# Moving 32 tokens of a mixture-of-neurons layer from gathered rows to dense products, and making fewer products ahead

## Chip, cores and metric

The kernel runs as one program on one core of a Trainium2 chip. The metric is the device time of one execution in microseconds (us), and the median over several executions is what is compared. Engines are named as in the profile: PE (TensorE matmuls), PEld (its weight loads), DVE (VectorE), ACT (ScalarE), POOL (GpSimd), SP (SyncE, which issues most DMAs).

## What is computed

Two layers of a diffusion backbone over 512 latent tokens (`x`) and 256 context tokens (`ctx`), width 1024, all in fp32. Each layer is a token mixer and then a channel mixer, "PEER", which is all that matters here. PEER picks for every token 8 x 16 = 128 of 16,384 single-neuron experts; each has a row `u` and a row `v` of 1024 numbers:

```python
qr = (h @ wq)...;  scores = einsum(qr, subkeys)        # 8 heads x 2 halves x 128 keys
s1, i1 = top_k(scores[..., 0, :], 16);  s2, i2 = top_k(scores[..., 1, :], 16)
top, pos = top_k(s1 + s2, 16)                          # of 256 pairs; expert = i1 * 128 + i2
gate = softmax(top)
act = gelu(einsum('ted,td->te', u[ek], hk))            # ek: the 128 experts of a token
y   = einsum('te,ted->td', gate * act, v[ek])
```

The first layer does this for latent and context tokens, the second for the latent tokens alone, since nothing reads its context stream afterwards.

## The kernel before, in words

Tokens stand in blocks of 128. In each layer `peer` (line 664 and on) treats some tokens as *dense* and some as *gathered*.

**Dense tokens.** For them the activations of all 16,384 experts are computed: for every pair of two 128-expert blocks (64 pairs in all), `experts_in` loads two tiles of `u`, splits each into a rounded high part (`whi`, ACT, L298) and a rest (`wlo`, DVE, L300), makes three products for each of 8 slices of the width (`mm3`, L307 to L309; 2 x 8 x 3 = 48 matmuls for a pair, whose moving operand is as wide as there are dense tokens) and applies gelu (ACT, L805). In `dense`, 16 groups of 8 expert blocks follow each other: for a group the activations `A` are multiplied by the gates (DVE, L829), split (ACT L832, DVE L833), and for each of 8 slices of the output a tile of `v` is loaded, split (L298, L300) and multiplied in 24 matmuls (L840 to L842; 192 a group), whose sum DVE adds to the residual (L844). So a layer has 64 x 48 = 3072 U matmuls and 16 x 192 = 3072 V matmuls.

The gates of dense tokens are a table, 16,384 x tokens, built in `gates` and written to memory (`gd`). A *quad* is 32 tokens of it: per token, ACT and DVE make two one-hot matrices (L775 to L786), PE multiplies them (L791, which the trace shows as two instructions each), ACT copies the result out (L792). `dense` reads the table back (`gt`, L818).

While the table is being built, `ahead(q)` computes, after each quad, some of the U products and writes their activations to memory (`ad`, L726); `dense` reads those back (L821) instead of computing them. `AHEAD` says how many of the 64 pairs are made ahead in each layer, and `AHEAD_SET` spreads them from pair 3 up to pair `SPAN`. The first three pairs (`FIRST`) are computed only after the last gate matmul (`issue_after(self.last_gate)`).

**Gathered tokens.** `gather_block` (L866 and on) fetches, for a block of tokens on 128 partitions, one expert row for each partition with an indirect DMA from POOL (L881, 512 KB each), first all `u` rows, each reduced against the token's own `h` on DVE (L888), then all `v` rows, each multiplied and added to `acc` (L897). At the end PE transposes `acc` and DVE adds it to the residual (L903 to L907). The buffers `gr` (3) and `gs` (1) hold rows in flight; the first 96 `u` rows of a block whose picks come early use `gr` alone.

In the second layer 352 tokens are dense (`nt = len(db) * P - r`, `r = REST[1] = 32`), the block of the last 128 tokens is gathered with 128 u and 128 v fetches, and the 32 tokens left over are gathered in a second, packed block: four groups of 32 partitions hold the same 32 tokens with a quarter of their experts each, so that 32 u and 32 v fetches do. In the first layer all 512 latent tokens are dense and the 256 context tokens gathered.

**What sets the order.** The program is written in the order above; a scheduler places every engine's instructions by a simulation of its own when the kernel is built, and each engine then runs its list in that fixed order. All DMAs but the gathers are issued by SP, in order.

```python
for i in range(q * n_ahead // n, (q + 1) * n_ahead // n):   # ahead(q); n = nt // 32 quads
    A = self.experts_in(l, ap, hx, AHEAD_SET[l][i], nt)
    nc.sync.dma_start(ad[i], A)
...
nq = (nt - n * P) // 32
self.gates(kp, gd, n, ahead, *sel, min(nq, P // 32))
...
if r:
    self.gather_block(l, cp, c2, hdx[0, P - r:], *rest, TC + nt, r, 0)
```

Of the kernel before, what the change touches and what calls it, by code (L numbers as in the profile page):

```python
# [32 lines left out]
TINY = 2.0 ** -60  # L33
HUGE = 1.0e37
WPRIO = 400
AHEAD = (36, 40)
SPAN = (39, 60)
FIRST = 3
AHEAD_SET = [[FIRST + i * (m - FIRST) // n for i in range(n)] for n, m in zip(AHEAD, SPAN)]
ND = 3  # L40
REST = (0, 32)
STEP = (-1, -1)
POOL_NM = False
U0 = 96
# [12 lines left out]
class Kern:  # L57
# [603 lines left out]
    def peer(self, l):  # L661
# [3 lines left out]
        db = [b for b in range(NCB, NB) if b not in gb]  # L665
        r = REST[l]
        nt = len(db) * P - r
        early = EARLY[l]
        with ExitStack() as es:
            dr = self.pool(f"dr{l}", stack=es, space=DRAM)  # L670
            gd = dr.tile([P // 4, P, nt // 32, 4, 32], F, name="gd")
            n_ahead = AHEAD[l]
            ad = dr.tile([n_ahead, P, 2, nt], F, name="ad")
# [330 lines left out]
```

## Time and profile before

| | us |
|---|---|
| median of 3 runs (lowest 4182.07, highest 4183.38) | 4182.8 |
| the profiled execution | 4198.16 |
| its span in the trace | 4196.4 |

| engine | busy us | share of the span |
|---|---|---|
| PE | 3905.2 | 93% |
| PEld | 3359.6 | 80% |
| DVE | 3399.4 | 81% |
| ACT | 1794.3 | 43% |
| POOL | 1391.9 | 33% |

The profiled execution took 15.4 us (0.4%) more than the median; all times that are read from the trace are its own. Times below are us from the start of the span. The second layer's channel mixer fills about the last 1,230 us of it: U products begin at about 2975, the table of gates is built from about 3070 to 3390, the dense groups run from there to 4158, and a final norm ends the span. A share of PE's busy time hides gaps between pipelined matmuls, so the steps from one matmul's start to the next's are read as well.

### The profile page before, as it was taken

The page shows a single profiled execution, that of the slowest core. Times are in us where ns is not written, and L with a number is a line of the kernel's source. Part 1 is how long each engine was busy: PE and PEld are TensorE (multiplying, and loading weights), DVE is VectorE, ACT ScalarE, POOL GpSimd, SP SyncE. Part 2 cuts the span into 40 slices and gives each one's busy share as a digit, 9 for nine tenths or more (in the row PEclk, how much of TensorE's full clock was granted, in tenths as well). Part 3 has the DMA queues.
Part 4 walks back from the last instruction along what each step waited for, and adds up shares of the span by engine and source line. Part 5 has one row for each costly group of instructions (what it writes and reads, how often), then busy time and mean ns, then how long its engine had stood idle before and what let it go on. Part 6 is the DMA issues. An engine that isn't in the chain of part 4 may idle for free. (4 is left out here: it accounts for less than half of the span.)

```text
span 4196.4 us, 59194 instructions
## 1 busy us (share of the span) xinstructions
PE 3905.2 (93%) x21317; PEld 3359.6 (80%) x21317; DVE 3399.4 (81%) x6491; ACT 1794.3 (43%) x3096; POOL 1391.9 (33%) x1020
## 2 busy tenths in 40 slices
PE   8999999989999999999999879988999999998898
PEld 5888779778888778877777658866899998888897
DVE  4766639989886999988888868757999888898897
ACT  4444332358985222222222335433387853333332
POOL 0211112033331335455555532212013333444443
PEclk8999999999999999999999989989999999999998
DMA  6444122389998899988899921112469999999996
GB/s 222 138 155 156 64 74 74 114 291 318 313 314 278 295 337 344 338 317 310 317 323 319 321 96 58 64 61 88 138 218 315 325 368 337 342 333 344 349 338 232
DMA packets 391173, 1021.28 MB, mean 243 GB/s; under 512 B 32096, under 2 KB 159328, under 8 KB 386528
## 3 DMA queue, kind: packets, MB, share of 16 engines
q1 hardware_dynamic: 271072, 581.24, 39.9%
q0 software_dynamic: 119808, 436.26, 29.3%
q8 instruction: 168, 2.75, 0.3%
q14 instruction: 125, 1.02, 0.1%
HBM read 918.00 MB, written 99.35 MB: 242 GB/s over the span
## 5 line engine op out<-in xcount | busy, mean ns | idle before, releaser
L298 ACT ACTIVATE whi<-wraw 128x1024 fp32r<-128x1024 f32 x624 | 656.5, 1058 | 1160.8 <-PE p L841 465.4
L881 POOL DMA_INDIRECT gr<-in_u,picki x360 | 486.9, 1353 | 968.0 <-DVE gr L888 640.9
L300 DVE TENSOR_TENSOR wlo<-wraw,whi 128x1024 fp32r<-128x1024 f32 x592 | 721.2, 1223 | 96.9 <-ACT whi L298 92.5
L840 PE MATMUL p<-Wh,whi 128*128 128x512 f32 (+1 forms) x2048 | 730.5, 364 | 46.2 <-ACT Wh L832 22.3
L841 PE MATMUL p<-Wl,whi 128*128 128x512 f32 (+1 forms) x2048 | 741.5, 363 | 26.1 <-DVE Wl L833 25.9
L842 PE MATMUL p<-Wh,wlo 128*128 128x512 f32 (+1 forms) x2048 | 740.5, 364 | 24.5 <-DVE wlo L300 23.4
L309 PE MATMUL p<-hxh,wlo 128*128 128x512 f32 (+1 forms) x2048 | 744.7, 364 | 9.3 <-DVE wlo L300 9.2
L307 PE MATMUL p<-hxh,whi 128*128 128x512 f32 (+1 forms) x2048 | 744.1, 363 | 3.0 <-ACT whi L298 2.6
L308 PE MATMUL p<-hxl,whi 128*128 128x512 f32 (+1 forms) x2048 | 743.3, 363 | 0.0
L881 POOL DMA_INDIRECT gr<-in_v,picki x312 | 443.5, 1421 | 469.4 <-DVE acc L897 359.5
L888 DVE SCALAR_TENSOR_TENSOR gr<-gr,htok 128x1024 f32<-128x1024 f32 x360 | 436.4, 1219 | 118.8 <-DMA gr<-in_u,picki 117.4
L840 PEld LDWEIGHTS p<-Wh,whi 128*128 128x128 f32 x2048 | 389.8, 192 | 100.9 <-ACT Wh L832 29.5
L842 PEld LDWEIGHTS p<-Wh,wlo 128*128 128x128 f32 x2048 | 392.2, 192 | 80.5 <-DVE wlo L300 40.4
L841 PEld LDWEIGHTS p<-Wl,whi 128*128 128x128 f32 x2048 | 393.4, 192 | 77.1 <-DVE Wl L833 36.3
L897 DVE SCALAR_TENSOR_TENSOR acc<-gr,gw,acc 128x1024 f32<-128x1024 f32 x308 | 394.1, 1280 | 54.0 <-DMA gr<-in_v,picki 51.6
L309 PEld LDWEIGHTS p<-hxh,wlo 128*128 128x128 f32 x2048 | 388.9, 190 | 50.3 <-DVE wlo L300 12.9
L307 PEld LDWEIGHTS p<-hxh,whi 128*128 128x128 f32 x2048 | 388.7, 190 | 42.1 <-ACT whi L298 4.1
L308 PEld LDWEIGHTS p<-hxl,whi 128*128 128x128 f32 x2048 | 388.8, 190 | 37.7
L832 ACT ACTIVATE Wh<-A 128x1024 fp32r<-128x1024 f32 (+1 forms) x128 | 118.1, 926 | 386.4 <-DVE A L829 305.1
L791 PEld LDWEIGHTS gps<-oA,oB 128*128 128x128 f32 x1728 | 240.2, 194 | 44.6 <-ACT oB L780 13.5
L791 PE MATMUL gps<-oA,oB 128*128 128x128 f32 x1728 | 251.3, 280 | 25.4 <-DVE oA L783 13.8
L307 PE MATMUL pj<-h512h,whi 128*128 128x512 f32 x640 | 261.9, 412 | 12.4 <-ACT h512h L368 3.2
(320 smaller groups left out, 6703.4 us busy)
## 6 DMA issues: line engine op xcount, KB each, us to landing
wraw<-in_ut SPq DMA_DIRECT2D x256, 512.0 KB, 6.2
wraw<-in_vt SPq DMA_DIRECT2D x256, 512.0 KB, 6.2
gd<-stg SPq DMA_DIRECT2D x27, 2048.0 KB, 13.5
wmod<-in_w_mod SPq DMA_DIRECT2D x96, 512.0 KB, 4.7
wraw<-in_w_in SPq DMA_DIRECT2D x64, 512.0 KB, 3.5
gt<-gd SPq DMA_DIRECT2D x32, 1024.0 KB, 8.3
gt<-gd SPq DMA_DIRECT2D x32, 704.0 KB, 7.8
ad<-A SPq DMA_DIRECT2D x36, 512.0 KB, 6.8
```

The source lines that it names most:

```text
L298: nc.scalar.activation(hi, raw, AF.Copy)
L300: (eng or nc.vector).tensor_tensor(lo, raw, hi.bitcast(F), op=OP.subtract)
L307: nc.tensor.matmul(out, wh[:, k], ah[:, k, :n], start=i == 0, stop=False)
L308: nc.tensor.matmul(out, wh[:, k], al[:, k, :n], start=False, stop=False)
L309: nc.tensor.matmul(out, wl[:, k], ah[:, k, :n], start=False, stop=i == KC - 1)
L791: mm = nc.tensor.matmul(pt[:, s], B[:, s4 + s], A[:, s4 + s], start=True, stop=True)
L840: nc.tensor.matmul(pt, hi[:, j], wh, start=j == 0, stop=False)
L841: nc.tensor.matmul(pt, hi[:, j], wl, start=False, stop=False)
L842: nc.tensor.matmul(pt, lo[:, j], wh, start=False, stop=j == NG - 1)
L881: nc.gpsimd.indirect_dma_start(out=t, out_offset=None, in_=src, in_offset=bass.IndirectOffsetOnAxis(ap=eidx[:, e:e + 1], axis=0))
L888: nc.vector.scalar_tensor_tensor(u, u, 1.0, htok, op0=OP.mult, op1=OP.mult, accum_out=act[:, e:e + 1])
L897: nc.vector.scalar_tensor_tensor(acc, v, w[:, e:e + 1], acc, op0=OP.mult, op1=OP.add)
```

## The change

`REST[1]` goes from 32 to 0: the second layer has 384 dense tokens (three whole blocks), 12 quads of gates and no packed second block of gathers. `AHEAD` goes from 36 and 40 pairs to 34 and 30, and the first layer's `SPAN` from 39 to 37, so that its pairs made ahead are 3 to 36 and no longer 3 to 38.

```diff
-AHEAD = (36, 40)
-SPAN = (39, 60)
+AHEAD = (34, 30)
+SPAN = (37, 60)
 FIRST = 3
 AHEAD_SET = [[FIRST + i * (m - FIRST) // n for i in range(n)] for n, m in zip(AHEAD, SPAN)]
 ND = 3
-REST = (0, 32)
+REST = (0, 0)
```

The numbers move instructions at three places that matter below.

PE, second layer, end of the building of gates (`p_...` are U products for pairs, `gps` the gate products). Before, with 40 pairs ahead, the last products of the table stand among U products:

```order
L791 MATMUL gps<-oA,oB 128x128 x2
L309 MATMUL p_28526<-hxh,wlo 128x352
L791 MATMUL gps<-oA,oB 128x128
L307 MATMUL p_28526<-hxh,whi 128x352
L791 MATMUL gps<-oA,oB 128x128 x4
L308 MATMUL p_28526<-hxl,whi 128x352
```

Now the last pair made ahead ends before them, and 128 tokens' products, four quads, stand in one piece:

```order
L307 MATMUL p_27988<-hxh,whi 128x384
L308 MATMUL p_27988<-hxl,whi 128x384
L309 MATMUL p_27988<-hxh,wlo 128x384
L761 MATMUL gtr<-ident,ix 128x128
L761 MATMUL gtr<-ident,gate 128x128
L791 MATMUL gps<-oA,oB 128x128 x128
L307 MATMUL p_28061<-hxh,whi 128x384
```

The U products behind that piece are those of the first three pairs, which wait for the last gate. Counted along the two lists, 33.0 pairs stood before the 256th token's product and 40 before the 352nd; now 29.8 stand before the 256th and 30 before all the rest.

ACT, the same place. Before, the splits and gelus of U products stand between the one-hot matrices:

```order
L780 ACTIVATE oB<-oB,gt_27528,gtn 128x128 x3
L792 ACTIVATE stg<-gps 128x128x4
L780 ACTIVATE oB<-oB,gt_27528,gtn 128x128 x2
L792 ACTIVATE stg<-gps 128x128x4
L298 ACTIVATE whi<-wraw 128x1024
L805 ACTIVATE A<-p_28526 128x704
```

Now the last four quads have ACT to themselves:

```order
L779 ACTIVATE oB<-iota,gt_26932 128x128 x5
L792 ACTIVATE stg<-gps 128x128x4 x2
L780 ACTIVATE oB<-oB,gt_26936,gtn 128x128 x5
L792 ACTIVATE stg<-gps 128x128x4 x2
L298 ACTIVATE whi<-wraw 128x1024 x2
L805 ACTIVATE A<-p_28061 128x768
```

DVE, end of the second layer. Before, additions of gathered rows (L897) run to the end, and the packed block's eight residual adds (L907) follow the last dense add (L844):

```order
L844 SCALAR_TENSOR_TENSOR resx<-p_34654,mod_114,resx 128x352
L897 SCALAR_TENSOR_TENSOR acc<-gr,gw,acc 128x1024 x2
L897 SCALAR_TENSOR_TENSOR acc<-gs,gw,acc 128x1024
L907 SCALAR_TENSOR_TENSOR resx<-accT,mod_114,resx 128x32 x8
L216 TENSOR_SCALAR fv<-nst_35741 128x4
```

Now the dense adds are the last:

```order
L300 TENSOR_TENSOR wlo<-wraw,whi 128x1024
L844 SCALAR_TENSOR_TENSOR resx<-p_34619,mod_114,resx 128x384
L844 SCALAR_TENSOR_TENSOR resx<-p_34651,mod_114,resx 128x384
L844 SCALAR_TENSOR_TENSOR resx<-p_34683,mod_114,resx 128x384
L844 SCALAR_TENSOR_TENSOR resx<-p_34715,mod_114,resx 128x384
L216 TENSOR_SCALAR fv<-nst_35576 128x4
```

In the new DVE list the last addition of a gathered row stands behind 80 of the layer's 128 dense adds, so 48 V tiles (six groups) come after it.

## Rows read from the trace of the kernel before

**Rows 1.** The page's first part: busy us (share of the span) and instructions of each engine.

```profile
span 4196.4 us, 59194 instructions
PE 3905.2 (93%) x21317; PEld 3359.6 (80%) x21317; DVE 3399.4 (81%) x6491; ACT 1794.3 (43%) x3096; POOL 1391.9 (33%) x1020
```

**Rows 2.** Busy time by stage, all engines: stretch, its length, then busy us (instructions) of PE, PEld, DVE, ACT and POOL, the granted clock as a share of 2.4 GHz, the DMA engines' busy share, GB/s. First the first layer's dense groups and its end, then the second layer: gates up to about the 256th token, the last 96 tokens, the dense groups, the end.

```profile
1400.00:2400.00 1000.00, 957.69 (x4125) 773.36 (x4124) 873.01 (x1013) 274.00 (x271) 520.47 (x358) 0.99 0.91 325
2400.00:2450.00 50.00, 23.47 (x67) 14.35 (x67) 37.86 (x45) 7.19 (x12) 24.54 (x17) 0.64 0.60 197
...
3060.00:3310.00 250.00, 236.83 (x1584) 232.25 (x1584) 220.09 (x410) 206.63 (x465) 60.50 (x48) 0.99 0.83 281
3310.00:3390.00 80.00, 80.00 (x562) 79.98 (x561) 67.09 (x120) 74.17 (x173) 28.02 (x20) 1.00 1.01 351
3390.00:4156.00 766.00, 708.38 (x4193) 684.25 (x4192) 670.81 (x782) 245.51 (x263) 340.45 (x251) 0.98 0.94 342
4156.00:4197.00 41.00, 20.52 (x64) 9.13 (x62) 14.45 (x27) 8.61 (x13) 1.88 (x1) 0.69 0.24 86
```

**Rows 3.** PE's instructions in order of time, where nothing interrupts them: start, duration, instruction. First 352 columns wide (48 steps lie between the two rows), then 512 wide (15 steps), then 256 wide (6 steps).

```profile
4110.26 0.32 PE L307 MATMUL p<-hxh,whi 128*128 128x352 f32 x1
...
4117.94 0.32 PE L307 MATMUL p<-hxh,whi 128*128 128x352 f32 x1
```

```profile
1700.09 0.39 PE L841 MATMUL p<-Wl,whi 128*128 128x512 f32 x1
...
1703.49 0.39 PE L841 MATMUL p<-Wl,whi 128*128 128x512 f32 x1
```

```profile
303.35 0.28 PE L309 MATMUL pj<-h256h,wlo 128*128 128x256 f32 x1
...
304.03 0.28 PE L309 MATMUL pj<-h256h,wlo 128*128 128x256 f32 x1
```

**Rows 4.** The same view of PE around 3164: twelve gate-product instructions (two for a token) and what starts behind them.

```profile
3164.08 1.50 PE L791 MATMUL gps<-oA,oB 128*128 128x128 f32 x12
3165.33 0.41 PE L307 MATMUL p<-hxh,whi 128*128 128x352 f32 x1
```

**Rows 5.** Groups of instructions by line and shape: count, then busy us, mean ns of one, then idle us of the engine before them and what ended it.

```profile
L780 ACT ACTIVATE oB<-oB,gt,gtn 128x128 f32<-128x128 f32 x540 | 227.7, 498 | 0.1
L779 ACT ACTIVATE oB<-iota,gt 128x128 f32<-128x128 f32 x540 | 171.3, 405 | 0.2
L792 ACT ACTIVATE stg<-gps 128x512 f32<-128x512 f32 x216 | 126.5, 596 | 34.5 <-PE gps L791 34.3
```

**Rows 6.** The stretch 3310 to 3390 alone, three times: the instructions of L791 (PE, PEld), of L298 (ACT) and of L805 (ACT).

```profile
3310.00:3390.00 80.00, 28.48 (x197) 26.91 (x195) 1.00 1.01 351
```

```profile
3310.00:3390.00 80.00, 16.26 (x16) 1.00 1.01 351
```

```profile
3310.00:3390.00 80.00, 6.06 (x8) 1.00 1.01 351
```

**Rows 7.** DMA in the dense groups of the second layer, 3400 to 4155: total, then issues by tile with their count, KB of each and the median us from issue to landing.

```profile
DMA packets 70774, 257.60 MB, mean 341 GB/s; under 512 B 7894, under 2 KB 7951, under 8 KB 70721
...
wraw<-in_vt SPq DMA_DIRECT2D x126, 512.0 KB, 6.4
gt<-gd SPq DMA_DIRECT2D x32, 704.0 KB, 7.8
wraw<-in_ut SPq DMA_DIRECT2D x42, 512.0 KB, 6.1
A<-ad SPq DMA_DIRECT2D x40, 352.0 KB, 8.7
```

**Rows 8.** Who PE waited for between 3400 and 4160: us in total, times, longest.

```profile
PE p L840 <- ACT Wh L832: 17.6, 14, 4.6
PE p L842 <- DVE wlo L300: 16.8, 15, 2.7
PE p L841 <- DVE Wl L833: 12.8, 13, 1.7
```

**Rows 9.** Busy time, columns as in Rows 2: forty microseconds without a gap on PE, and ten with one.

```profile
4110.00:4150.00 40.00, 40.00 (x252) 40.00 (x251) 38.12 (x38) 14.83 (x16) 22.76 (x15) 1.00 0.91 314
3540.00:3550.00 10.00, 6.41 (x37) 5.55 (x35) 6.97 (x12) 2.49 (x3) 4.29 (x3) 1.00 1.00 368
```

**Rows 10.** PE in order of time at the end of the second layer, with the idle time before and what ended it: the last V matmul and the first transposition of the packed block's sum.

```profile
4158.14 0.32 PE L842 MATMUL p<-Wh,wlo 128*128 128x352 f32 x1
4164.02 0.63 PE L905 MATMUL accT<-pack,acc 128*128 128x32 f32 x2 [5.56 <-DVE acc L897]
```

**Rows 11.** The chain that ended last, its final stretch: start, us, what. The norm's column sums (L242) stand between the transpositions, then the norm's end.

```profile
4165.65 1.92 PE nst L242 x2
...
4180.51 1.07 PE nst L250 x8
```

**Rows 12.** The end of the first layer: its last V matmul, and the last addition of a gathered row.

```profile
2389.94 0.39 PE L842 MATMUL p<-Wh,wlo 128*128 128x512 f32 x1
```

```profile
2443.22 1.28 DVE L897 SCALAR_TENSOR_TENSOR acc<-gs,gw,acc 128x1024 f32<-128x1024 f32 x1 [1.06 <-DMA gs<-in_v,picki]
```

## Prediction

> **What bounds the kernel now.** I read the busy shares first [rows 1]: PE 93%, DVE 81%, too near each other to name a bound for the whole span. The table by stage comes next [rows 2]. In the second layer's dense groups (3390 to 4156) PE is busy 708 of 766 us, DVE 671, and the DMA engines 94% of the time: three resources near their limit at once. While the table of gates is built, PE and ACT are: in its last 80 us PE 80.0 and ACT 74.2. PE's busy time hides how fast matmuls follow each other, so I take the step from start to start [rows 3]: 48 steps in 7.68 us at 352 columns, 160 ns each; 15 in 3.40 us at 512, 227 ns; 6 in 0.68 us at 256, 113 ns. PE's work in a stage is a count times such a step; what the stage takes beyond that I call its loss.
>
> The dense groups hold 24 pairs not made ahead (24 x 48 = 1152 U matmuls) and 3072 V matmuls: 4224 x 0.160 = 676 us. They last from 3390 to the last V matmul's end, 4158 [rows 10], so 768 us, and the loss is 92. The waits say through whom it comes: ACT's and DVE's splits arrive late [rows 8], and in a stretch with a gap on PE the DMA engines stand at 1.00 and DVE at 7.0 of 10 us, so there nobody computes and data are late [rows 9].
>
> **The change, part by part.** Terms are against the profiled execution, 4198.2 us, which is 15.4 over the median; I carry the difference over to the median as it is.
>
> *Wider matmuls.* All 6144 matmuls of the second layer's dense part go from 352 to 384 columns. No row shows 384. Between the steps at 352 and 512 a column costs 67/160 = 0.42 ns, between 256 and 352 0.49 ns, so 384 takes 173.4 to 175.7 ns. I take 173.4, since the 512 row is the same kind of stream. That is 13.4 ns x 6144 = 82 us more PE work, whatever stage it falls in.
>
> The Trainium skill says otherwise: its page "TensorE: Matmul & The Clock Gate", section Back-to-back issue gap, gives for sustained pairs of weight load and matmul 81 ns at 128 columns and 131 ns at 512. An estimate from those two figures is 4.2 ns for 32 columns, 26 us in all, and with it the sum below would come to about +12 instead. This trace does not agree with it: 512 columns take 227 ns here.
>
> *Gates.* There are 12 quads instead of 11, and 30 pairs beside them instead of 40. By the instruction order PE has 29.8 pairs ahead of the 256th token, before 33.0: 29.8 x 48 x 0.1734 = 248 us against 253, so that point, now at about 3310 (510 gate products, two a token, lie before it [rows 2, 6]), comes 5 us earlier. After it the order holds 128 tokens' gate products in one piece with no U product between. PE needs 256 x 0.104 = 27 us for them [rows 4]; ACT sets the pace. From below: in 3310 to 3390 ACT was busy 74.2 us, of which 16.3 + 6.1 were splits and gelus, so 51.9 us for 98.5 tokens [rows 2, 6], 67 us for 128. From above: 20 x 0.405 + 20 x 0.498 + 8 x 0.596 = 22.8 us a quad [rows 5], 91 us. I take 80, between them, because PE and ACT now wait for each other with no other work to fill in. Gates end at 3305 + 80 = 3385: **-5** (bounds -18 and +6). PE stands idle for some 50 of those 80 us, and its clock may fall; gate products at half the clock would take 53 us and still be hidden.
>
> *Dense groups.* Ten pairs fewer were made ahead, so 34 x 48 + 3072 = 4704 matmuls remain: 4704 x 0.1734 = 816 us against 676, **+140**. About 80 of these are the pairs moved here, 58 the wider columns.
>
> *Their loss.* The packed block's 64 gathers go (33.6 MB, and 64 passes of DVE). Twenty U tiles come in (10.5 MB), readback and gate tables change by -2.6 and +2.1 MB [rows 7], and seven gathers more are done before the gates end (69 against 62 in DVE's order): some 230 MB instead of 257.6. The relief is uneven: in the new order the 187 gathers left all lie ahead of the 80th of 128 V tiles. Up to there PE has 1968 V and about 960 U matmuls, 508 us; DMA has 82 V and 40 U tiles, 187 gathers, 20 gate tables and 19 readbacks, some 186 MB, at the 341 GB/s that this stage reached [rows 7] 545 us. So 37 us of loss there. Behind it nothing competes: I put 10 us for the start of the stage and all the rest, as 4110 to 4150 shows PE without a gap even with gathers beside it [rows 9]. Loss 47 instead of 92: **-45** (bounds: 15, if PE runs as in that row, and 92, if nothing is gained).
>
> *End.* From the last V matmul's end (4158.5) to the end of the span there are now 38 us: 5.6 for the last gathered sum, then eight transpositions each followed by a norm's column sum, and from 4180.5 on 16 us that stay [rows 10, 11]. Without the packed block only the last dense add, its square and the last sums precede those 16; 6 us, six of the 0.96 us that a sum takes in rows 11. **-16** (bounds -20, if they are nearly hidden, and -10).
>
> *First layer.* Two pairs, 2 x 48 x 0.227 = 22 us of PE, go from its gates to its dense groups. The layer ends with gathers 54 us after its last V matmul [rows 12], so that a later end of the groups is covered. What is saved is 2.1 MB of activations written and read, 6 us at 325 GB/s [rows 2], if DMA paces the gathers. **-5** (bounds -20, PE's time leaving the gates in full, and +10, half of it coming back through the gathers).
>
> The rest (wider passes over `A` on DVE and ACT, 64 fewer issues on POOL, fewer on SP) lies beside these. Sum: -5 + 140 - 45 - 16 - 5 = **+69 us**: 4267 for a profiled execution, **4252 for the median**.
>
> **Rivals.**
> *No relief* (0.15). DVE still carries gathers, splits and residual adds in a fixed order, and where they meet, PE waits as now. For it: DVE was busy 38.1 of 40 us even in the good stretch [rows 9]. Then the loss stays 92: +114, 4297.
> *Full relief* (0.13). ACT runs the last quads in 67 us and the dense loss falls to 15: -13 - 32 more, +24, 4207. Against it: 186 MB have to pass in 508 us, 366 GB/s, in the contended part, more than this stage's 341 [rows 7].
> *The other side: weight loads pace the stream* (0.04). In 4110 to 4150 PEld is busy 40.00 of 40 us [rows 9]. If loads set the 160 ns, 384 columns cost no more than 352: dense groups 4704 x 0.160 + 10 = 763 (-5), gates 29.8 x 48 x 0.0134 = 19 us earlier still (-24), end -16, first layer -5: -50, 4133. It turns from slower to faster at a step of 168 ns: there 4704 and 1430 matmuls at that step, a loss of 10 and the two savings balance. Against it: 256 columns follow each other in 113 ns with the same 128x128 loads [rows 3]. The Trainium skill's page "Perfetto Trace Analysis", section Identifying the Most-Contended Engine, does tell one to judge PE by the busy share of its weight loads and not of its matmuls; the row at 256 columns is why I don't follow it here.
> That the change doesn't do what it says is excluded by the new order, which holds 384-wide products and no packed block.
>
> **How the numbers follow.** My forecast, +42 to +97 around 4252, gets 0.62; its own range, 4225 to 4280, is the loss between 25 and 70 with the gates' bounds. The rivals have 0.15, 0.13 and 0.04, and 0.06 is left for what I haven't thought of, either way. The range **4210 to 4300** takes in the forecast, the case of no relief and the better part of full relief. A measurement of this kernel tells about 0.2% (8 us) from no change. Slower by more: forecast, no relief, nearly all of full relief and some of the rest, 0.91. Within: 0.04. Faster: the weight loads and a little of the rest, 0.05.
>
> **What would show it.** In the profile after: a step of 173 ns at 384 columns; gates ending between 3372 and 3396, with ACT over 90% and PE's busy share well under half in the last 80 us; dense groups about 863 us long (816 and 47), with gaps on PE in their first 545 us only; 22 us from the last V matmul to the end; the first layer's end within 20 us of now. A step near 160 ns, or a dense stage under 790 us, would make the prediction wrong; gaps on PE also after the last gathered row would mean that the loss has another cause than DMA and gathers.

## The result

The changed kernel takes 4235.5 us (median of 4 runs, 4228.89 to 4239.53) against 4183.1 for the kernel before (4 runs): a ratio of 1.0118, 95% interval 1.0097 to 1.0139, so it is slower by some 50 us. Forecast were 4252 and a range of 4210 to 4300. The profiled execution took 4236.98, so this trace stands for the median; that of before was 15 us over its own, so two traces differ by 39 us where the medians differ by 52. A second profile of before is among the experiments for that reason.

### The profile page after: what moved, and what is told of

Read it like the earlier page. It is cut to its first block, busy times and chain, and to the rows that moved or that the text cites. A ratio compares the mean times of both kernels' runs of the same rounds, so it can differ in the third digit from the quotient of the medians.

```text
span 4235.2 us, 59025 instructions
## 1 busy us (share of the span) xinstructions
PE 3979.6 (94%) x21357; PEld 3450.1 (81%) x21357; DVE 3347.0 (79%) x6404; ACT 1818.4 (43%) x3143; POOL 1311.0 (31%) x956
## 5 line engine op out<-in xcount | busy, mean ns | idle before, releaser
L298 ACT ACTIVATE whi<-wraw 128x1024 fp32r<-128x1024 f32 x624 | 657.6, 1059 | 1285.4 <-PE p L841 589.0
L309 PE MATMUL p<-hxh,wlo 128*128 128x512 f32 (+1 forms) x2048 | 754.6, 369 | 7.1 <-DVE wlo L300 7.0
L307 PE MATMUL p<-hxh,whi 128*128 128x512 f32 (+1 forms) x2048 | 753.6, 368 | 0.4 <-ACT A L805 0.4
L308 PE MATMUL p<-hxl,whi 128*128 128x512 f32 (+1 forms) x2048 | 753.1, 368 | 0.0
L881 POOL DMA_INDIRECT gr<-in_u,picki x336 | 456.6, 1359 | 871.8 <-DVE gr L888 558.4
L881 POOL DMA_INDIRECT gr<-in_v,picki x288 | 408.3, 1418 | 408.1 <-DVE acc L897 310.1
L888 DVE SCALAR_TENSOR_TENSOR gr<-gr,htok 128x1024 f32<-128x1024 f32 x336 | 407.7, 1221 | 118.2 <-DMA gr<-in_u,picki 117.7
L897 DVE SCALAR_TENSOR_TENSOR acc<-gr,gw,acc 128x1024 f32<-128x1024 f32 x285 | 365.1, 1281 | 48.4 <-DMA gr<-in_v,picki 46.9
L791 PE MATMUL gps<-oA,oB 128*128 128x128 f32 x1792 | 275.8, 294 | 52.2 <-DVE oA L783 25.4
L791 PEld LDWEIGHTS gps<-oA,oB 128*128 128x128 f32 x1792 | 261.1, 205 | 77.4 <-ACT oB L780 32.7
```

The costliest lines, as they stand in the source:

```text
L298: nc.scalar.activation(hi, raw, AF.Copy)
L307: nc.tensor.matmul(out, wh[:, k], ah[:, k, :n], start=i == 0, stop=False)
L308: nc.tensor.matmul(out, wh[:, k], al[:, k, :n], start=False, stop=False)
L309: nc.tensor.matmul(out, wl[:, k], ah[:, k, :n], start=False, stop=i == KC - 1)
L791: mm = nc.tensor.matmul(pt[:, s], B[:, s4 + s], A[:, s4 + s], start=True, stop=True)
L881: nc.gpsimd.indirect_dma_start(out=t, out_offset=None, in_=src, in_offset=bass.IndirectOffsetOnAxis(ap=eidx[:, e:e + 1], axis=0))
```

## Profile after

The page's first part, against [rows 1]: PE has 74 us more, DVE 52 less, POOL 81 less.

```profile
span 4235.2 us, 59025 instructions
PE 3979.6 (94%) x21357; PEld 3450.1 (81%) x21357; DVE 3347.0 (79%) x6404; ACT 1818.4 (43%) x3143; POOL 1311.0 (31%) x956
```

Busy time by stage, columns as in [rows 2]: the first layer's end; the second layer's gates up to about the 256th token; its last 128 tokens; the dense groups as long as gathered rows come; the dense groups without them; the end.

```profile
2390.00:2450.00 60.00, 45.22 (x175) 29.71 (x174) 39.64 (x66) 21.89 (x45) 11.66 (x13) 0.80 0.36 115
3045.00:3273.00 228.00, 217.82 (x1416) 214.88 (x1414) 205.84 (x382) 197.05 (x447) 66.11 (x50) 0.99 0.87 296
3273.00:3355.00 82.00, 50.93 (x258) 44.39 (x259) 59.49 (x128) 69.52 (x192) 34.54 (x25) 0.73 0.83 269
3355.00:3906.00 551.00, 527.08 (x2952) 513.84 (x2952) 479.86 (x526) 175.81 (x186) 262.39 (x183) 0.99 0.93 342
3906.00:4211.00 305.00, 305.00 (x1762) 304.52 (x1760) 158.52 (x174) 103.74 (x109) 0.00 (x0) 1.00 0.45 156
4211.00:4235.00 24.00, 8.93 (x33) 3.71 (x32) 7.04 (x14) 7.02 (x11) 0.00 (x0) 0.70 0.24 87
```

The fourth and fifth rows are the reading that matters. While gathered rows come, the DMA engines are busy 93% of the time at 342 GB/s and PE has gaps; from 3906 on, POOL does nothing, the transfers fall to 156 GB/s, and PE is busy 305.00 of 305 us. The third row holds the last four quads, without U products beside them: PE is busy 62% of it, at a granted clock of 0.73.

PE in order of time at the end of the dense groups (start, duration, instruction): 48 steps between the first two rows, then the last V matmul and the norm's first column sums.

```profile
4200.56 0.33 PE L840 MATMUL p<-Wh,whi 128*128 128x384 f32 x1
...
4208.88 0.33 PE L840 MATMUL p<-Wh,whi 128*128 128x384 f32 x1
...
4210.79 0.34 PE L842 MATMUL p<-Wh,wlo 128*128 128x384 f32 x1
4211.06 1.05 PE L242 MATMUL nst<-sq,ones 128*32 128x512 f32 x4
```

48 steps in 8.32 us are 173.3 ns, against 160 at 352 columns [rows 3]. No transposition of a packed sum stands between the last V matmul and the sums any more [rows 10].

Who PE waited for in the dense groups, 3355 to 4212, against [rows 8] (us, times, longest): these three come to 20.9 us, against 47.2.

```profile
PE p L841 <- DVE Wl L833: 10.2, 11, 1.4
PE p L842 <- DVE wlo L300: 5.7, 12, 1.6
PE p L840 <- ACT Wh L832: 5.0, 5, 2.3
```

The first layer's last V matmul and its last addition of a gathered row, against [rows 12].

```profile
2387.47 0.39 PE L842 MATMUL p<-Wh,wlo 128*128 128x512 f32 x1
```

```profile
2418.80 1.28 DVE L897 SCALAR_TENSOR_TENSOR acc<-gs,gw,acc 128x1024 f32<-128x1024 f32 x1
```

The V matmuls end 2.5 us earlier than before, the rows 24.4 earlier.

## The experiments

Stage times of every kernel, each from its own profile, in us. "Rows" is the end of the first layer's last row addition, "start" the first U matmul of the second layer. "Gates" run from that start to the last gate product, "dense" from there to the last V matmul's end, "end" from there to the end of the span. The ratio is to runs of before on the same chip, whose medians lay between 4183 and 4189.

| kernel | columns; pairs ahead | rows | start | gates | dense | end | ratio (95%) |
|---|---|---|---|---|---|---|---|
| before | 352; 36, 40 | 2444 | 2969 | 417 | 773 | 38 | 1 |
| before again | same | 2436 | 2959 | 416 | 779 | 36 | |
| changed | 384; 34, 30 | 2420 | 2946 | 409 | 856 | 24 | 1.0118 (1.0097 to 1.0139) |
| e1 first layer alone | 352; 34, 40 | 2417 | 2940 | 416 | 776 | 37 | 0.9960 (0.9944 to 0.9977) |
| e2 second layer alone | 384; 36, 30 | 2439 | 2960 | 410 | 850 | 24 | 1.0148 (1.0126 to 1.0170) |
| e3 | 384; 34, 40 | 2417 | 2940 | 430 | 809 | 24 | 1.0046 (1.0026 to 1.0067) |
| e4 | 352; 34, 30 | 2423 | 2949 | 387 | 820 | 24 | 0.9975 (0.9958 to 0.9993) |
| e5 matmuls narrow | 384; 34, 30 | 2415 | 2936 | 406 | 805 | 24 | 0.9989 (0.9973 to 1.0004) |
| e6 half rows | 384; 34, 30 | 2419 | 2941 | 411 | 850 | 24 | 1.0116 (1.0094 to 1.0138) |
| e8 | 352; 32, 40 | 2423 | 2961 | 417 | 768 | 35 | 1.0001 (0.9986 to 1.0015) |
| e9 half passes | 384; 34, 30 | 2426 | 2950 | 414 | 843 | 24 | 1.0087 (1.0070 to 1.0104) |
| e10 two buffers | 384; 34, 30 | 2425 | 2951 | 418 | 945 | 24 | 1.0330 (1.0309 to 1.0351) |
| e11 | 352; 34, 36 | 2425 | 2952 | 400 | 781 | 29 | 0.9908 (0.9891 to 0.9925) |

The same stage differs between profiles of kernels that have it alike: the start by up to 15 us (2959 to 2969 in the three with 36 pairs, 2936 to 2952 in the nine with 34), the second layer's dense groups by up to 11 (768 to 779 in before, its repeat, e1 and e8). So a single difference of that size between two traces decides nothing.

### Before, a second time

The program of the kernel before, unchanged.

> The kernel before, unchanged, for a second profile of it: the first profiled execution was 15 us over its median. If those 15 us are spread over the program, each stage is as long within 5 us; if a stage holds them, a comparison of two traces misjudges that stage by as much. The unchanged halves of the first two runs make the first layer's end of the first profile 6 us later than its repeat, and the second layer's dense groups 4 us shorter.

It took 4191.28 us. The first layer's rows end at 2436 and the second layer starts 10 us earlier than in the first profile; its dense groups are 6 longer. So a part of the 24 us that the first layer seemed to gain belonged to the first profile: over the three kernels with 36 pairs and the nine with 34 the mean start is 2963.0 and 2944.9, 18 us apart.

### e1 and e2: one layer's part alone

```diff
 e1
-AHEAD = (36, 40)
-SPAN = (39, 60)
+AHEAD = (34, 40)
+SPAN = (37, 60)
 e2
-AHEAD = (36, 40)
+AHEAD = (36, 30)
-REST = (0, 32)
+REST = (0, 0)
```

> The kernel before with 34 instead of 36 pairs made ahead in the first layer and nothing else; the second layer is as before. In DVE's order 12 gathered rows are left to add behind the first layer's last dense add, before 24. Theory A: each row left there costs its own 2 us, because nothing is beside it; the layer ends 24 us earlier and the kernel takes 4159 us. Theory B, the prediction's term: only the 2.1 MB of activations written and read back are saved, 5 us, 4178; then the 24 us between the two traces are a difference of executions. Under both the second layer's stages last as in the kernel before (dense groups 768 us, end 38).

> The kernel before with the second layer of the change (384 dense tokens, 30 pairs ahead) and the first layer as before. Theory A: the second layer alone costs what the change cost and the 24 us that the first layer gave: 4235 + 24 = 4259 us. Theory B (first layer worth 5): 4240. Under both the dense groups last 856 us, the end 24, and the building of gates is about 8 shorter than before.

By the ratios the first layer alone is worth 0.40% of 4186 us, -17 (-23 to -10); the second alone costs 1.48%, +62. Together that makes +45, and the change measured +49. Both signs are real: the change is a gain of 17 and a loss of 62 in one. Theory A's -24 was too much and the prediction's -5 too little.

### e8: further on in the first layer

```diff
-AHEAD = (36, 40)
-SPAN = (39, 60)
+AHEAD = (32, 40)
+SPAN = (35, 60)
```

> The kernel before with 32 pairs made ahead in the first layer (SPAN 35), where the first run of this study had 34; the second layer is as before. In DVE's order one gathered row is left to add behind the first layer's last dense add, not 12. Theory A: in the run with 34 the rows left ran for 32 us behind the last V matmul, and with one left about 8 remain, so the layer ends 20 us or more earlier if the dense groups keep their end: 4148 us. Theory B: the dense groups already carry 325 GB/s, and the 11 rows and the two pairs that go into them lengthen them by as much, 5.8 MB or 18 us; 4168, as with 34.

The gain of e1 is gone again. PE in order of time in e8, its last V matmul of the first layer; then DVE's last addition of a row:

```profile
2419.09 0.39 PE L842 MATMUL p<-Wh,wlo 128*128 128x512 f32 x1
```

```profile
2421.68 1.28 DVE L897 SCALAR_TENSOR_TENSOR acc<-gs,gw,acc 128x1024 f32<-128x1024 f32 x1
```

The last addition starts 2.6 us behind the last V matmul, as the order said, but the V matmuls end 35 us later than in e1 (2419.5 against 2384.8): 22 of that is the two pairs' PE work, the rest loss. The building of gates did not get shorter (last gate product at 1298.6, in e1 at 1298.8). So the count of rows that the order leaves behind the last dense add does not by itself give the time (theory A fails). B is nearer: the dense groups do get longer, by twice what it said. What fits all profiles, though no run tests it alone, is a layer with two ends: the second layer's first U matmul came 521 to 527 us behind the last row wherever that stood 30 us or more behind the last V matmul, but in e8 538 behind it, since there the last V matmul is late (542 before the U matmul; 555 in e1). In the trace of the changed kernel the next layer's normalisation of the latent tokens (L271, L289) already runs on DVE between the last additions of rows. From 36 to 34 pairs the rows' end comes 19 us earlier in the mean (over the three and the nine profiles) and the V matmuls' end 5 us later; from 34 to 32 the other end becomes the later one.

### e3 and e4: width and pairs ahead, each alone

```diff
 e3, against the changed kernel
-AHEAD = (34, 30)
+AHEAD = (34, 40)
 e4, against the changed kernel
-REST = (0, 0)
+REST = (0, 32)
```

> The changed kernel with 40 pairs ahead in the second layer instead of 30 (first layer as changed, 384 dense tokens). PE's order has 29.8 pairs before the 256th token as in the change, and the other 10 among the last 128 tokens. Theory A (PE's work sets the dense groups wherever the DMA doesn't): 480 matmuls of 0.173 us leave the dense groups, -83, and some 7 of the loss with the 20 U tiles; in the last 128 tokens PE has 83 + 27 us of work where it now takes 82, so the gates end 30 us later. Sum -60, 4175 us. Theory B (the loss is a cost of the gates and pairs meeting, or ACT is the bound of the gates with the splits added): gates end 50 or more later and the gain is under 40, over 4195.

> The changed kernel with 352 dense tokens and the packed block kept, so only the 34 and 30 pairs of the change: against the first run of this set (352 tokens, 34 and 40 pairs) ten pairs move from the gates to the dense groups. Gates: 3 pairs fewer before the 256th token, -23, and the last 96 tokens without U products at 80/128 us each, 60 instead of 75, -15. Theory A (in the kernel before the transfers set the dense groups: 257.6 MB at 341 GB/s are 755 of their 768 us, and PE's 92 us of loss are its waiting for them): the stage carries some 269 MB, 790 us, and most of the 77 us of PE's work falls into gaps, +27. Sum -11: 4148 us if the first layer gives its 24. Theory B (the loss is PE's own and stays 92): dense groups 845 us, +77 - 38 = +39 against the first run, 4198.

With e1 and the changed kernel these are the four corners, all with 34 pairs in the first layer: 0.9960 (352, 40), 0.9975 (352, 30), 1.0046 (384, 40), 1.0118 (384, 30). Making ten pairs fewer costs 6 us at 352 columns and 30 at 384; the 32 columns cost 36 us with 40 pairs and 60 with 30. So most of the slowdown is the wider part, and the two don't add up. The stage times tell where the 24 us between 6 and 30 come from. Ten pairs fewer shorten the gates by 29 us at 352 columns and by 21 at 384, and they lengthen the dense groups by nearly the same, 44 and 47. The end is the larger difference: at 352 columns it shrinks from 37 us to 24, at 384 it was 24 already. In e1 PE waits for the packed block's last row behind the last V matmul; in e4, which keeps the packed block, its last row is added 23 us before the V matmuls end. PE in order of time at the end of e1's dense groups, then the last row addition and the last V matmul of e4:

```profile
4132.30 0.32 PE L842 MATMUL p<-Wh,wlo 128*128 128x352 f32 x1
4137.33 0.64 PE L905 MATMUL accT<-pack,acc 128*128 128x32 f32 x2 [4.71 <-DVE acc L897]
```

```profile
4132.96 1.29 DVE L897 SCALAR_TENSOR_TENSOR acc<-gs,gw,acc 128x1024 f32<-128x1024 f32 x1
```

```profile
4156.93 0.32 PE L842 MATMUL p<-Wh,wlo 128*128 128x352 f32 x1
```

PE's work in the dense groups grows by 77 us from e1 to e4 and by 69 from e3 to the changed kernel (in e3's order 1.7 of the 40 pairs stand behind the last gate product), so in both a part of it, 33 and 22 us, goes into gaps. For the dense groups theory A had 90 us in e3 and 27 in e4, and both were wrong. Theory B's time for e3 came true (4203.9 us, over 4195), but the gates end 21 us later than in the changed kernel and not 50; its 845 us for e4 were 820.

Where the gathered rows come, four rows are compared, columns as in [rows 2]: e1, e4 and e11 (below), with 352 columns, then e3 with 384.

```profile
3356.00:4132.00 776.00, 717.29 (x4232) 694.71 (x4231) 675.99 (x789) 247.65 (x266) 338.29 (x253) 0.97 0.93 340
```

```profile
3337.00:4134.00 797.00, 760.26 (x4577) 742.16 (x4576) 695.74 (x802) 267.59 (x289) 358.20 (x257) 0.99 0.94 340
```

```profile
3352.00:4130.00 778.00, 730.74 (x4406) 707.88 (x4405) 691.07 (x804) 256.63 (x276) 355.07 (x257) 0.99 0.94 344
```

```profile
3369.00:3945.00 576.00, 542.76 (x3007) 527.05 (x3006) 496.63 (x547) 181.02 (x191) 256.88 (x181) 0.98 0.94 343
```

The last column hardly moves: 340 to 344 GB/s, as 342 in the changed kernel, whatever PE has to do. At that rate the stretch lasts about as long as its bytes need (e1: 776 us at 340 GB/s are 264 MB), and PE's work that is moved into it fills gaps: the first four of the ten pairs, from e1 to e11, lengthen the dense groups by 5 us for 31 us more of PE's work. The other six, from e11 to e4, lengthen them by 39 us for 46 us of work: the rows now end before the V matmuls, and what stands behind them lies bare. With 384 columns the rows end early in any case, and PE runs 305 us without a gap behind them in the changed kernel. These are steps between single traces, so the sizes are good to some 10 us.

### e5: what the columns cost

All but the first of each 24 dense matmuls of an accumulation write 352 of the 384 columns; 32 tokens' sums are left incomplete (m is 352; one line is shown, and the other U matmuls and the V matmuls are cut alike).

```diff
-nc.tensor.matmul(out, wh[:, k], al[:, k, :n], ...)
+nc.tensor.matmul(out[:, :m], wh[:, k], al[:, k, :n][:, :m], ...)
```

> The changed kernel with the second layer's dense matmuls only 352 columns wide, all but the first of each accumulation of 24, while every table, pass over activations, split and transfer keeps its 384 columns; 32 tokens' sums are left incomplete. The prediction's step (13.4 ns of PE for 32 columns): 6144 x 23/24 x 0.0134 = 79 us of PE's work go, 18 of them before the gates end and 60 in the dense groups, of which the transfers hold back little, since the order lets the gathers run on to the 93rd V tile; 4235 - 75 = 4160 us, between 4150 and 4170. By the rival that weight loads pace the stream the step stays and so does the time, 4235. By the page of the Trainium skill on TensorE (TensorE: Matmul & The Clock Gate, Back-to-back issue gap) 32 columns are an estimated 4.2 ns, -25, 4210.

Against the changed kernel the ratio falls by 0.0129, 54 us. So the step does depend on the columns and PE's time does reach the end: the rival that weight loads pace the stream is out. The estimate of 25 us from the Trainium skill's page "TensorE: Matmul & The Clock Gate", section Back-to-back issue gap, does not agree with it either. But 54 is less than 75. The dense groups give 51 of the 60 us expected of them (45 against e2, which has the same second layer as the change). The gates give 4 of 18, within what two traces differ by; there ACT was busy 197 of 228 us in the changed kernel and would be the next to set the pace, which no run tested. Nor is e5 a test of the columns alone: its order runs the gathered rows on to the 93rd V tile and not the 80th.

### e6 and e9: transfers or passes on DVE

e6 fetches v rows of half the length and reads the half twice; e9 fetches whole rows and multiplies and adds half of each, which leaves half of the gathered sum's columns incomplete. Of e6 only the line that names the rows is shown; the other changed lines fill half of the buffer and read it twice.

```diff
 e6
-            v = fetch(a[f"v{l}"], e)
+            v = fetch(a[f"v{l}"].rearrange("n (a b) -> (n a) b", a=2) if l else a[f"v{l}"], e)
 e9
-nc.vector.scalar_tensor_tensor(acc, v, w[:, e:e + 1], acc, ...)
+nc.vector.scalar_tensor_tensor(acc[:, :512 * (2 - l)], v[:, :512 * (2 - l)], w[:, e:e + 1], acc[:, :512 * (2 - l)], ...)
```

> The changed kernel with the second layer's 128 gathered v rows fetched at half their length (256 KB a fetch and not 512, other rows), while DVE's passes keep their 1024 elements by reading the half twice; so 33.6 MB of transfers go and no instruction of another engine. In the order the last gathered addition stands at the 72nd V tile, not the 80th. Theory A (the transfers set the contended part: there 188.4 MB passed at 342 GB/s in 551 us, while PE had 508 us of work): up to the 72nd tile some 149 MB, 435 us, lie under PE's 458, so that the loss of 41 us falls to about 10; 4205 us. Theory B (the passes on DVE between the splits make PE wait): the passes are the same, 4235.

> The changed kernel with full fetches, while DVE's passes over the second layer's gathered v rows (all but the first) take only half of each row, so that the sum is complete in 512 of 1024 columns; some 127 x 0.6 = 76 us of DVE's work go from the contended part and no transfer, and the order keeps the last gathered addition at the 80th V tile. The half-row run left the time where it was, with DVE busy 48 of 50 us in place of the transfers at their limit, so either of the two could hold the stage. Theory A (with full rows the transfers do: 188 MB at 342 GB/s): 4235 us, loss 41. Theory B (the passes hold the splits up at either transfer rate): the loss falls to some 15, 4210. Theory C (both matter about equally, each wait being for the later of the two): half of that, 4220.

The half rows left the time where it was (1.0116 against 1.0118), where the transfers as the only cause asked for -30. Fifty microseconds of v rows in the changed kernel, in e6 and in e9:

```profile
3700.00:3750.00 50.00, 45.29 (x256) 44.00 (x256) 43.28 (x43) 13.89 (x15) 25.21 (x20) 1.00 0.93 337
```

```profile
3700.00:3750.00 50.00, 48.99 (x281) 48.20 (x280) 48.48 (x48) 16.23 (x17) 28.73 (x20) 1.00 0.82 269
```

```profile
3700.00:3750.00 50.00, 48.81 (x278) 47.56 (x276) 36.74 (x45) 17.31 (x18) 20.64 (x19) 1.00 0.96 358
```

With half the bytes the transfers fall to 269 GB/s and DVE is busy 48.5 of 50 us (third number); with half the passes DVE falls to 36.7 and the transfers rise to 358 GB/s. This looks like two limits close together, each of which takes over when the other is eased; it is read from the rows and not shown by a run of its own. e6 isn't a clean test, because its order also packs the rows closer, ending at the 72nd V tile, which puts more DVE work into each microsecond. e9's order keeps the 80th tile, and it gives 13 us (1.0118 to 1.0087). The two intervals overlap, and the two ratios are from different series of runs; its dense groups are 843 us long, against 856 and 850 in the changed kernel and e2. Its rows' stretch:

```profile
3365.00:3904.00 539.00, 525.73 (x2969) 514.18 (x2969) 418.73 (x527) 176.88 (x186) 223.19 (x182) 1.00 0.95 351
```

539 us for 189.0 MB, against 551 for 188.4. PE's 2969 matmuls at 173.4 ns are 515 us, so 24 us of loss stay with 61 us less on DVE, where the changed kernel has 39 and e2, with the same second layer, 34. That is nearest to theory C: 10 to 15 us of the loss go with DVE's passes, and most of it stays. That the rest belongs to the transfers is argued and not shown.

### e10: fewer fetches in flight

```diff
-t = cp.tile([P, D], F, name="gr", tag="gr", bufs=3)
+t = cp.tile([P, D], F, name="gr", tag="gr", bufs=3 - l)
```

> The changed kernel with two buffers instead of three for the second layer's gathered rows, so that fewer fetches are in flight; work and bytes are the same. The order spreads the gathers to the 92nd of 128 V tiles, not the 80th. Theory A (the loss is what the contended part's bytes exceed PE's work by): up to the 92nd tile some 205 MB, 600 us at 342 GB/s, meet 584 us of PE's work instead of 545 against 508, so the loss falls from 41 to about 25; 4220 us. Theory B (each gathered row costs PE its share of delay wherever it stands, 41 us for 183 rows): 4235 as now.

Both theories fail: the kernel loses another 90 us. From 3368 to 4085, while its rows come, the busy times (columns as above) and then DVE's longest waits (us, times, longest):

```profile
3368.00:4085.00 717.00, 641.91 (x3395) 619.09 (x3395) 532.12 (x590) 203.76 (x215) 265.19 (x192) 0.93 0.82 288
```

```profile
DVE acc L897 <- DMA gr<-in_v,picki: 84.7, 42, 6.8
DVE gr L888 <- DMA gr<-in_u,picki: 78.8, 39, 4.5
```

The transfers reach only 288 GB/s, so it is no lack of bandwidth. With fewer fetches in flight rows come later than the order has them, and DVE stands 163 us in front of rows that haven't come, against 25 while rows come in the changed kernel. Behind them in its list stand the splits, and PE waits for those: a piece of DVE's list, with the idle time before a row and what ended it,

```profile
3700.17 1.28 DVE L897 SCALAR_TENSOR_TENSOR acc<-gs,gw,acc 128x1024 f32<-128x1024 f32 x1
3704.59 1.28 DVE L897 SCALAR_TENSOR_TENSOR acc<-gr,gw,acc 128x1024 f32<-128x1024 f32 x1 [3.14 <-DMA gr<-in_v,picki]
3705.79 1.14 DVE L844 SCALAR_TENSOR_TENSOR resx<-p,mod,resx 128x384 f32<-128x384 f32 x2
3706.85 2.35 DVE L300 TENSOR_TENSOR wlo<-wraw,whi 128x1024 fp32r<-128x1024 f32 x2
```

and PE's waits for them, in the same stretch:

```profile
PE p L842 <- DVE wlo L300: 35.2, 23, 6.6
PE p L841 <- DVE Wl L833: 14.6, 10, 2.8
```

This is the path by which a late row costs PE time, and the same two waits lead the list of the changed kernel at 5.7 and 10.2 us. Bytes and DVE's load would act through it too, by which e6 and e9 can be understood, but no run shows that apart. No run had more than three of these buffers, so whether the 342 GB/s are the most that such transfers reach or what this number of fetches in flight gives is open.

### e11: a version that beats both

```diff
-AHEAD = (36, 40)
-SPAN = (39, 60)
+AHEAD = (34, 36)
+SPAN = (37, 60)
```

> The kernel before with 34 and 36 pairs ahead, 352 dense tokens and the packed block kept: between the runs of 34 and 40 pairs (4168 us) and of 34 and 30 (4173). With 40 the gathered rows end 4 us after the last V matmul and 37 us follow it; with 30 they end 23 us before it and 24 follow. If the two trends are straight lines, the time lies between, 4170; if the best lies where rows and V matmuls end together, the end is 12 us shorter at little more PE work, 4160.

4152.0 us, 0.9908 of before (0.9891 to 0.9925): 22 us better than e1 by the ratios, where 8 were hoped for. In its profile the gates are 16 us shorter than e1's, the dense groups 5 longer for 31 us more of PE's work (the row above: 344 GB/s), and the end 8 shorter, because the last row is added 4 us before the last V matmul ends and no longer 5 behind it. So a few pairs fewer ahead, with 352 tokens, is the part of this change worth keeping. A neighbour such as 35 or 37 pairs wasn't tried.

## Why the prediction was right

The sign and the range held, and the largest term was the right one: the kernel is slower because the dense groups get more PE work, by ten pairs and by 32 columns, than the relief in transfers gives back. The sizes of two terms were off. By its steps:

- **Wider matmuls.** 173.4 ns forecast, 173.3 in the trace. The Trainium skill's page "TensorE: Matmul & The Clock Gate", section Back-to-back issue gap, would have 4.2 ns for the 32 columns by the estimate in the prediction; this trace shows 13.3, and in e5 taking the columns away gives 54 us. The forecast let PE's work reach the end in full, which was a third too much (54 of 79 us, with e5's other order in it).
- **Gates, -5.** They take 409 us and 410 in e2, against 417 and 416: -7, within the bounds. The last 128 tokens took 82 us for the 80 forecast. ACT is busy in 69.5 of them, 85% and not over 90, and PE 62% and not well under half: at a granted clock of 0.73 its gate products kept it busy for 51 us, where 27 were reckoned at the full clock. Neither cost anything that shows.
- **Dense groups, +140 - 45.** As a length 863 was forecast, and 856 measured (850 in e2). As a difference +95 was forecast, and +77 measured. PE's work was right (815 - 676 = +139). The relief was sized too small: the loss was to fall from 92 to 47, and it fell from 100 to 38 (means of the two profiles each), -62 and not -45. "Full relief" (a loss of 15) and "no relief" (92) are both out. The forecast's split held: 545 us with 186 MB at 341 GB/s, where the trace has 551 with 188.4 at 342, then no gap.
- **What the loss is** was told too simply: transfers alone. e6 and e9 point to DVE's passes as a second limit close behind, and e10 shows a path from a late row to PE. "No relief" named DVE's fixed order; in that it was partly right, in its size not.
- **End, -16.** 24 us after 38 and 36: -13. But the reason given, that the packed block is gone, is not the one that counts: e4 keeps the packed block and ends in 24 us as well, because its last row comes before the last V matmul.
- **First layer, -5**, with bounds of -20 and +10: e1 gives -17 by time. The prediction saw the 54 us of rows behind the last V matmul, and took them to be a cover for a later end of the groups; that fewer rows are left there (12 and not 24 in DVE's order) and that the second layer starts earlier with their end (18 us in the mean), it did not cost.

The sum by the measured terms: -17 for the first layer, -7 for the gates, +77 for the dense groups, -13 for the end (the last three as means of the changed kernel and e2 against the two profiles of before): +40 against +49 by the ratio. The 9 left over are no more than what traces of one kernel differ by in a stage. The forecast's +69 lies 29 over that sum, 18 of it in the dense groups and 12 in the first layer. Both misses go the same way, so no luck hides in the sum; against the measured +49 the forecast is 20 too high.

## What to carry to other kernels

Find for each stage what a second resource needs in that stretch (bytes by the rate that the stage reaches), and move work on the first only as long as the second is the longer: four pairs moved into the dense groups cost 5 us there while gathered rows ran to their end, and six more cost 39. Look at a stage's ends as well: the ten pairs cost 6 us in all where they also took 13 from the end, and 30 where the end was short already. In a list of fixed order count what stands behind a transfer that can be late. Work out the two halves of an edit apart: here one half was a gain, and with a better number (e11) it beats both kernels.

## What the runs showed of the hardware

While gathered rows came in the second layer's dense groups, the transfers' rate was 339 to 351 GB/s over the whole stretch in ten kernels with full rows and three buffers, at 93 to 95% busy DMA engines, though PE's matmuls filled between 87 and 95% of it; with two buffers in place of three for the rows it was 288 at 82%. Matmuls with a new weight load each went in steps of 173.3 ns at 384 columns, on the line between 160 at 352 and 227 at 512 [rows 3].
